# Convolution phases between the sections of attention, transfers of the bias frames on another queue, and part of the ConvFFN's operands made by token tile

## The chip, the cores and the metric

One core of one Trainium2 chip runs the whole layer in one launch. The metric is the device time of that launch in microseconds, from three runs: 1868.3, 1868.54 and 1870.0 us, median 1868.54 us.

## What is computed

One trunk layer over 1024 latent tokens (a grid of 16 rows and 64 columns) and 256 context tokens, 1024 wide, float32. Half of the mixing width is attention with 8 heads, the other half a bidirectional long convolution ("Hyena"). Cut to what matters here:

```python
h = rmsnorm(x, norm1_g) * (1 + sc1) + sh1
proj = h @ w_in                       # q, k, v and three Hyena inputs
a = attend(q, k, v)                   # latent: window 8 x 16 with a bias by
                                      # relative position, and all context keys
x1, x2, v = split(dwconv3(proj[..., 3 * 512:]))
z = x1 * long_conv(v, k_f[0])         # FFT convolution, filters from a small net
hyo = x2 * long_conv(z, k_f[1])
x = x + g1 * (concat(rmsnorm(a), rmsnorm(hyo)) @ w_out)
h2 = rmsnorm(x, norm2_g) * (1 + sc2) + sh2
gate, up = split(dwconv3(h2 @ w_up))  # 2 * 2816 columns
x = x + g2 * ((silu(gate) * up) @ w_down)
y = rmsnorm(x, final_g)
```

## The kernel before

All matrix products of weights run as three products of halves: each float32 operand is split into a rounded high part and the rest (`mm3`, lines 115 to 118). ACT rounds the high part, and DVE or GpSimd (POOL in the profile) subtracts for the low one.

The kernel is written in a framework with tiles and pools. The program emits instructions in its own order; a list scheduler then sets the order on each engine's queue from data dependences and priorities. What is emitted inside `tc.high_priority` is drawn forward by the offset given there. A pool opened with `reuse_waits="tile"` lets each tile start as soon as the old tiles in its place are done with. On the chip each engine and each queue of DMA issues (SP, POOL, ACT) works in order.

The stages, on the time axis of the profile:

- **To some 570 us, filters and input projections.** PE makes the products with w_in (bank `psp`, 512 latent or 256 context columns at a time) for the Hyena inputs, then for q, k and v. Beside them the filters are made on DVE, GpSimd and ACT (helpers at lines 371 to 470; `csl`, `cs`, `GO`, `GE` and `cc` are their tiles), stored as spectra `Kd`. Among the Hyena chunks `rpb_frames` (lines 547 to 558) runs three times: it fills a frame with 16 small loads of the bias table (line 556), reorders it by a copy (557) and stores it to the DRAM table `rpw` (558).
- **448 to 793 us, the convolution** (`chain`, from line 771). Five chains, four for 128 latent channels each and one for the context, of eight phases each: for each of the two convolutions a forward transform on PE (bank `pscA`, line 804, with the table `dftf`; input `s` loaded from `lxd` by line 790), sums of it and the product with the spectrum `K` on DVE, the inverse sums with rotations on ACT and DVE, and the inverse transform (line 876, table `idft`) with the gates. The result goes to the DRAM tensor `hyd`. Two lanes, chains 0, 2, 4 and chains 1, 3, take turns phase by phase. The first 16 phases have three PSUM banks, the other 24 one. All 40 are emitted in a row before the attention, at high priority.
- **597 to 869 us, the attention** (`attend`, from line 1030) for four pairs of heads. Each pair goes through blocks of queries: scores on PE (bank `psS`, line 1047), the bias added with a maximum on DVE (line 1068, tables `tb` 0 to 2), exponentials on ACT, transposes on PE (bank `psX`, line 1091) with evictions on ACT and DVE, and products with the values (bank `psav`, line 1008). The tables of a pair are 48 loads from `rpw` on GpSimd's queue (line 960).
- **880 to 1015 us, the output projection.** w_out is loaded by SP (line 1175, tile `wor`), scaled and split (lines 1167 and 1168). Ten groups of 128 tokens each go through the product with w_out (`omm`, bank `psd`), the residual, the norm and a transpose into `hA` (columns of the first part, 256) and `hB` (the second part, 384) (`post`, line 1315; last multiply at line 1342).
- **From 1015 us, the ConvFFN.** Its product with w_up is a block scheme of seven products in place of eight, with seven sums of w_up's blocks on the left and seven sums `Ta`, `Tb` of blocks of `hA`, `hB` on the right. `first_operands` (line 1347) makes four of the seven steps of the first part inside the loop over token groups; the rest of `Ta` and all of `Tb` come behind the loop (lines 1393 to 1416; subtractions on tiles `T` at line 1233, sums `tsb`). The first sum of w_up's blocks on DVE is line 1478 (tile `S`), and its products go to the banks `psa`, `psb` and `psc`.

The emission of the phases and of the attention before:

```python
for n, i in enumerate(turn2):          # 40 phases in a row
    if n == 16:
        cbk.close()
        cbk = Banks("bkd", "right", "tile", cA=(1, 1))
    with tc.high_priority(offset=CHP):
        next(lanes[i], None)
...
for p_ in range(4):
    attend(p_)
```

Of the kernel before, what the change touches and what calls it, by code (L numbers as in the profile page):

```python
# [19 lines left out]
P = 128  # L20
# [66 lines left out]
def _build(nc, tc, top, V, A, G, T, Q, I, O, dbg, upto):  # L87
# [462 lines left out]
    def rpb_frames(t, var):  # L550
# [214 lines left out]
    Q.dma_start(out=dftf.rearrange("p a b -> p (a b)"), in_=I["t_dft"].flatten().rearrange("(p x) -> p x", p=P))  # L765
    Q.dma_start(out=idft.rearrange("p a b c -> p (a b c)"), in_=I["t_idft"].flatten().rearrange("(p x) -> p x", p=P))
# [135 lines left out]
    turn2 = [0, 0] + [1, 0] * 20 + [0] * 8  # L902
    for n, i in enumerate(turn2):
        if n == 16:
            cbk.close()
            cbk = Banks("bkd", "right", "tile", cA=(1, 1))
        with tc.high_priority(offset=CHP):
            next(lanes[i], None)
# [41 lines left out]

    def bias_load(p_, var):

        for half in range(2):
            for rq in range(8):
# [5 lines left out]
                G.dma_start(out=tv[:, :, a * 8:a * 8 + 64],  # L960
                            in_=rpw[var, :, 2 * p_:2 * p_ + 2, :, d * 8:d * 8 + 64].rearrange("q h u x -> q (h u) x"))
# [9 lines left out]
    for var in range(3):  # L971
        G.memset(tbs[var], NEG)
        bias_load(0, var)
        if var == 0:
            for r in Pring:
                for t in r:
                    G.memset(t[:, 0, :, 11:16], 0.0)
                    G.memset(t[:, 1, :, 0:4], 0.0)

# [50 lines left out]
    def attend(p_):  # L1030

        q, k = qkload(p_) if p_ else first
        vs = tp.tile([P, 12, P], F32, tag="vs", name="vs", bufs=2)
        G.dma_start(out=vs[:, 0:10], in_=vd[:, :, p_ * P:(p_ + 1) * P].rearrange("n p x -> p n x"))
        for h in range(2):
            G.dma_start(out=vs[:, 10:12, h * DH:(h + 1) * DH],
                        in_=I["cache_ctx_v"][0, 0, 2 * p_ + h].rearrange("(n p) d -> p n d", p=P))
        if p_:
            for var in range(3):
                bias_load(p_, var)  # L1040
# [82 lines left out]
        for b in range(2):  # L1123
            l, l2 = stat("l", 8), stat("l2", 8)
            for j in range(2):
                scores(2 * b + j, l, l2, j)
            V.tensor_add(l, l, l2)
            av = bk("av")
            for j in range(2):
# [4 lines left out]
                for vt, ps in local(cb):  # L1134
# [3 lines left out]
                         bs.rearrange("p (b r c) -> p b r c", b=2, r=16))  # L1138
        if p_ < 3:
# [6 lines left out]
    for p_ in range(4):  # L1146
        attend(p_)
# [8 lines left out]
    wsrc = I["w_out"][0].rearrange("(k p) c -> p k c", p=P)  # L1156
    wes = ExitStack()
# [633 lines left out]
```

## Time and profile before

| | |
|---|---|
| median of three runs | 1868.54 us |
| profiled execution | 1868.46 us |
| its span, first to last instruction | 1866.7 us |
| mean granted TensorE clock | 0.963 of full speed |
| PE busy, matmuls | 1728.6 us (93%) |
| DVE busy | 1365.0 us (73%) |
| ACT busy | 891.3 us (48%) |
| POOL busy | 366.3 us (20%) |
| DMA | 249.76 MB, mean 134 GB/s |

The span is what the trace covers; the execution's own time lies 1.8 us above it. PE are matmuls, PEld the loads of their weights, which overlap them. The granted clock is the share of full speed (2.4 GHz) that the chip let TensorE have, averaged over a stretch; the clock has two levels, 1.2 and 2.4 GHz, so 0.75 means half of the stretch at each. SPq and POOL in lists of transfers are the engines that issue them. In rows of waits, "A <- B" reads: A stood idle until B released it.

### The profile page before, as it was taken

The page shows a single profiled execution, that of the slowest core. Times are in us where ns is not written, and L with a number is a line of the kernel's source. Part 1 is how long each engine was busy: PE and PEld are TensorE (multiplying, and loading weights), DVE is VectorE, ACT ScalarE, POOL GpSimd, SP SyncE. Part 2 cuts the span into 40 slices and gives each one's busy share as a digit, 9 for nine tenths or more (in the row PEclk, how much of TensorE's full clock was granted, in tenths as well). Part 3 has the DMA queues.
Part 4 walks back from the last instruction along what each step waited for, and adds up shares of the span by engine and source line. Part 5 has one row for each costly group of instructions (what it writes and reads, how often), then busy time and mean ns, then how long its engine had stood idle before and what let it go on. Part 6 is the DMA issues. An engine that isn't in the chain of part 4 may idle for free.

```text
span 1866.7 us, 27362 instructions
## 1 busy us (share of the span) xinstructions
PE 1728.6 (93%) x9999; PEld 1453.5 (78%) x9999; DVE 1365.0 (73%) x2158; ACT 891.3 (48%) x1852; POOL 366.3 (20%) x436
## 2 busy tenths in 40 slices
PE   5899999999995688988997899999999999999997
PEld 2688778787884445656886899999999999788786
DVE  4668957852987898762466888889878777666797
ACT  4655545443342466673555444344444444443452
POOL 2356656531114555310110000000000000000001
PEclk7999999999997699998999899999999999999999
DMA  7424354356546234331331445554221222844653
GB/s 271 139 77 138 114 164 131 111 138 203 165 141 200 68 99 134 93 111 59 112 113 57 129 151 167 172 169 158 82 66 57 74 74 95 320 141 127 210 191 130
DMA packets 207289, 249.76 MB, mean 134 GB/s; under 512 B 26915, under 2 KB 152980, under 8 KB 206898
## 3 DMA queue, kind: packets, MB, share of 16 engines
q1 hardware_dynamic: 196936, 231.86, 38.5%
q0 software_dynamic: 8512, 15.33, 3.4%
q8 instruction: 79, 1.29, 0.3%
q10 hardware_dynamic: 1705, 0.82, 0.2%
q14 instruction: 57, 0.46, 0.1%
HBM read 176.75 MB, written 71.20 MB: 133 GB/s over the span
## 4 chain that ended last, share of the span: by engine, by line
PE 50%; DVE 22%; DMA 12%; issue 6%; ACT 6%; POOL 2%; SPq 1%; DVEq 0%; ACTq 0%; POOLq 0%
PE psd L116 6%; PE psd L117 6%; PE psd L118 6%; PE psp L116 2%; PE psp L118 2%; PE psp L117 2%; PE psa L116 2%; PE psa L117 2%; PE psa L118 2%; DMA wt<-in_w_down_dram 2%; DMA tdr<-wt 2%; PE psc L117 2%; PE psc L118 2%; PE psc L116 2%; PE psav L1008 1%
## 5 line engine op out<-in xcount | busy, mean ns | idle before, releaser
L116 PE MATMUL psp<-hh,wh 128*128 128x512 f32 (+1 forms) x552 | 201.6, 365 | 1.9 <-ACT wh L121 1.9
L117 PE MATMUL psp<-hl,wh 128*128 128x512 f32 (+1 forms) x552 | 199.0, 361 | 0.0
L118 PE MATMUL psp<-hh,wl 128*128 128x512 f32 (+1 forms) x552 | 198.1, 360 | 0.0
L116 PE MATMUL psa<-T,ws 128*128 128x256 f32 (+1 forms) x528 | 166.0, 314 | 5.6 <-ACT rows L1506 5.4
L117 PE MATMUL psa<-T,ws 128*128 128x256 f32 (+1 forms) x528 | 165.3, 313 | 2.9 <-DVE T L1233 2.9
L1706 POOL TENSOR_TENSOR rs<-rs,mhalf 128x1 f32<-128x1 f32 x10 | 7.7, 770 | 815.3 <-DVE rs L1705 815.3
L118 PE MATMUL psa<-T,ws 128*128 128x256 f32 (+1 forms) x528 | 164.7, 312 | 0.0
L116 PE MATMUL psd<-wd,gs 128*128 128x512 f32 x360 | 140.8, 392 | 3.1 <-ACT gs L121 3.1
L117 PE MATMUL psd<-wd,gs 128*128 128x512 f32 x360 | 141.0, 392 | 0.0
L118 PE MATMUL psd<-wd,gs 128*128 128x512 f32 x360 | 124.9, 390 | 1.8 <-DVE gs L122 1.8
L116 PEld LDWEIGHTS psp<-hh,wh 128*128 128x128 f32 x552 | 104.9, 190 | 22.8 <-issue 7.0
L116 PE MATMUL psc<-T,ws 128*128 128x384 f32 (+1 forms) x352 | 110.0, 313 | 7.8 <-ACT ws L121 7.8
L118 PEld LDWEIGHTS psp<-hh,wl 128*128 128x128 f32 x552 | 104.6, 189 | 15.5 <-issue 1.2
L117 PEld LDWEIGHTS psp<-hl,wh 128*128 128x128 f32 x552 | 105.1, 190 | 14.0 <-issue 0.4
L960 POOL DMA_DIRECT2D tb<-rpw x192 | 100.2, 530 | 78.2 <-DVE m L1068 60.5
L117 PE MATMUL psb<-T,ws 128*128 128x384 f32 (+1 forms) x352 | 109.8, 312 | 0.5 <-DVE T L1233 0.5
L117 PE MATMUL psc<-T,ws 128*128 128x384 f32 (+1 forms) x352 | 110.1, 313 | 0.0
L116 PE MATMUL psb<-T,ws 128*128 128x384 f32 (+1 forms) x352 | 109.4, 311 | 0.4 <-ACT T L1232 0.4
L118 PE MATMUL psc<-T,ws 128*128 128x384 f32 (+1 forms) x352 | 109.7, 312 | 0.0
L118 PE MATMUL psb<-T,ws 128*128 128x384 f32 (+1 forms) x352 | 109.5, 311 | 0.0
L116 PEld LDWEIGHTS psa<-T,ws 128*128 128x128 f32 x528 | 101.1, 192 | 7.4 <-ACT rows L1506 7.4
L117 PEld LDWEIGHTS psa<-T,ws 128*128 128x128 f32 x528 | 101.2, 192 | 3.1 <-DVE T L1233 3.1
(394 smaller groups left out, 4753.1 us busy)
## 6 DMA issues: line engine op xcount, KB each, us to landing
wada<-in_w_ada_dram SPq DMA_DIRECT2D x48, 512.0 KB
wr<-in_w_up_dram SPq DMA_DIRECT2D x44, 512.0 KB
gr<-gdr SPq DMA_DIRECT2D x44, 320.0 KB
wr<-in_w_in_dram SPq DMA_DIRECT2D x23, 512.0 KB
wt<-in_w_down_dram SPq DMA_DIRECT2D x44, 256.0 KB
tdr<-wt SPq DMA_DIRECT2D x44, 256.0 KB
gdr<-cv SPq DMA_DIRECT2D x22, 512.0 KB
wr<-tdr SPq DMA_DIRECT2D x20, 512.0 KB
```

What stands on the lines that cost most here:

```text
L116: T.matmul(out, ah, bh, start=start, stop=False, skip_group_check=True)
L117: T.matmul(out, ah, bl, start=False, stop=False, skip_group_check=True)
L118: T.matmul(out, al, bh, start=False, stop=stop, skip_group_check=True)
L960: G.dma_start(out=tv[:, :, a * 8:a * 8 + 64], in_=rpw[var, :, 2 * p_:2 * p_ + 2, :, d * 8:d * 8 + 64].rearrange("q h u x -> q (h u) x"))
L1008: T.matmul(av[h * DH:(h + 1) * DH, c0:c0 + 256], vt[:, h * DH:(h + 1) * DH], p[:, h * 256:(h + 1) * 256], start=start, stop=False, tile_po ...
L1706: G.tensor_tensor(rs, rs, mhalf, op=ALU.pow)
```

## The change

1. The 51 transfers of `rpb_frames` are issued by GpSimd and not by SP.
2. The loads of the chain's tables `dftf` and `idft` get high priority.
3. Only the first 16 phases of the convolution are emitted in a row at high priority, with three banks. The other 24 are emitted between parts of the attention at ordinary priority: `attend` becomes a generator that stops three times in each pair (after the scores of either half, and after the first half's result), and after the stops two, one and two phases are emitted, after the pair two more; the phases that are left over run out in the last pair. The table of turns is shortened to the 40 phases that there are.
4. All loads of the second pair (`q`, `k`, `vs`, bias tables), and the bias loads of the later pairs, are issued behind the last bias load of the first pair. This sets the order of issue alone.
5. The split halves of the first three of w_out's eight blocks live in a pool `tp0` with two places, `T0` and `T1`. The same places then take `Tb[0]` and `Tb[1]`. Four block sums of the second part are computed 128 columns at a time inside the loop over token groups (`second_sums`, groups 7 to 9), the sum for `Tb[6]` in place; `Tb[0]` and `Tb[1]` are split in the loop too. Behind the loop there remain the splits of `Ta[4]`, `Tb[4]`, `Ta[5]`, `Tb[5]`, `Tb[2]`, `Ta[6]`, `Ta[3]`, `Tb[6]`, `Tb[3]`.

The arithmetic is the same, apart from the tiles of item 5 being smaller. The core of the diff:

```diff
@@ rpb_frames
-            Q.dma_start(out=fv[cq * 8:cq * 8 + 8, :, a:a + 16], in_=I["rpb"][0][:, :, a + 7 - cq:a + 23 - cq])
+            G.dma_start(out=fv[cq * 8:cq * 8 + 8, :, a:a + 16], in_=I["rpb"][0][:, :, a + 7 - cq:a + 23 - cq])
...
-        Q.dma_start(out=rpw[var].rearrange("q h u x -> (q h) (u x)"), in_=g)
+        G.dma_start(out=rpw[var].rearrange("q h u x -> (q h) (u x)"), in_=g)
@@ tables of the chain
+    with tc.high_priority(offset=2000):
+        Q.dma_start(out=dftf..., in_=I["t_dft"]...)
+        Q.dma_start(out=idft..., in_=I["t_idft"]...)
@@ phases
-    turn2 = [0, 0] + [1, 0] * 20 + [0] * 8
-    for n, i in enumerate(turn2):
...
+    turn2 = [0, 0] + [1, 0] * 16 + [0] * 6
+
+    def phases(n):
+        for _ in range(n):
+            if turn2:
+                next(lanes[turn2.pop(0)], None)
+
+    with tc.high_priority(offset=CHP):
+        phases(16)
+    cbk.close()
+    cbk = Banks("bkd", "right", "tile", cA=(1, 1))
@@ attend
+        with tc.issue_after(blast0) if p_ == 1 else ExitStack():
+            q, k = qkload(p_) if p_ else first
...
         if p_:
-            for var in range(3):
-                bias_load(p_, var)
+            with tc.issue_after(blast0):
+                for var in range(3):
+                    bias_load(p_, var)
...
                 scores(2 * b + j, l, l2, j)
+            yield
             V.tensor_add(l, l, l2)
...
+            if b == 0:
+                yield
...
     for p_ in range(4):
-        attend(p_)
+        for n, _ in enumerate(attend(p_)):
+            phases(2 - n % 2)
+        phases(2)
@@ w_out
+    f0s = ExitStack()
+    tp0 = pool(f0s, "Tb0", side="right", reuse_waits="tile")
+    wfirst = [tp0.tile([P, 3, D], F32R, tag=f"T{p}", name=f"w{p}", bufs=1) for p in (0, 1)]
...
-                hi, lo = [wo_.tile([P, D], F32R, tag=f"w{x}{k}", name=f"w{x}{k}", bufs=1) for x in "hl"]
+                hi, lo = [wfirst[i // 3][:, i % 3] for i in (2 * k, 2 * k + 1)] if k < 3 else \
+                    [wo_.tile([P, D], F32R, tag=f"w{x}{k}", name=f"w{x}{k}", bufs=1) for x in "hl"]
@@ operands of the second part
+    def second_sums(t):
+        cs = slice(t * P, (t + 1) * P)
+        if t == 0:
+            ts = acp.tile([P, 3, 4, NS[1]], F32, tag="acc", name="tsb", bufs=1)
+            b.update({4: ts[:, 0], 5: ts[:, 1], 3: ts[:, 2]})
+        V.tensor_sub(b[4][..., cs], b12[..., cs], b11[..., cs])
+        V.tensor_sub(b[5][..., cs], b22[..., cs], b[4][..., cs])
+        V.tensor_sub(b[3][..., cs], b21[..., cs], b[5][..., cs])
+        V.tensor_sub(b12[..., cs], b22[..., cs], b12[..., cs])
...
+        if n >= 7:
+            second_sums(n - 7)
+        if n in (7, 8):
+            Tb[n - 7] = operand(tp0, n - 7, NS[1])
+            osplit(Tb[n - 7], b[n - 7])
...
-    osplit(Tb[0], b[0])
-    osplit(Tb[1], b[1])
-    V.tensor_sub(b[4], b12, b11)
-    a_operand(4)
-    osplit(Tb[4], b[4])
-    V.tensor_sub(b[5], b22, b[4])
-    a_operand(5)
-    osplit(Tb[5], b[5])
-    V.tensor_sub(b[3], b21, b[5])
+    for p in (4, 5):
+        a_operand(p)
+        osplit(Tb[p], b[p])
     osplit(Tb[2], b[2])
-    V.tensor_sub(b[6], b22, b12)
     a_operand(6)
     a_operand(3)
```

Three places where the order on an engine's queue differs. Lines after the change are some 11 to 30 higher than before from the attention on, and one higher in the chain.

**GpSimd, last of the three frames.** Before, between the frame's fill (L552) and its copy (L557) stand filter operations (L394 to L461); the loads are not on this queue:

```order
L552 MEMSET rp 128x480
L455 TENSOR_TENSOR GO<-GO 128x2x2x128
L394 TENSOR_TENSOR cs_2415<-sd_2403,sd_2394 128x512
L395 TENSOR_TENSOR cs_2415<-sd_2403,sd_2394 128x512
L460 TENSOR_TENSOR GE<-cc,GO 128x2x256
L461 TENSOR_TENSOR cc<-cc,GO 128x512
L557 COPY rp<-rp 128x15x4x8
L394 TENSOR_TENSOR cs_2494<-sd_2482,sd_2473 128x512
L395 TENSOR_TENSOR cs_2494<-sd_2482,sd_2473 128x512
```

And after the change:

```order
L552 MEMSET rp 128x480
L556 DMA rp<-in_rpb_dram 8x15x16 x13
L455 TENSOR_TENSOR GO<-GO 128x2x2x128
L556 DMA rp<-in_rpb_dram 8x15x16
L394 TENSOR_TENSOR cs_2415<-sd_2403,sd_2394 128x512
L395 TENSOR_TENSOR cs_2415<-sd_2403,sd_2394 128x512
L556 DMA rp<-in_rpb_dram 8x15x16 x2
L460 TENSOR_TENSOR GE<-cc,GO 128x2x256
L557 COPY rp<-rp 128x15x4x8
L461 TENSOR_TENSOR cc<-cc,GO 128x512
L122 TENSOR_TENSOR wl<-wr,wh 128x1024
L558 DMA rpw<-rp 128x480
```

The 16 loads of the frame (13, then 1, then 2) now stand among the filter operations, 13 of them ahead of `GO`, and the store L558 follows on the same queue.

**PE, first scores of the attention.** `s_...` with `dftf` or `idft` are products of the chain, `psS` scores, `psX` transposes of the attention. Before:

```order
L876 MATMUL pscA<-s_5623,idft 128x256 x4
L1047 MATMUL psS<-k,q 128x264 x2
L1047 MATMUL psS<-k,q 128x288 x2
L804 MATMUL pscA<-s_5863,dftf 128x256 x4
L1047 MATMUL psS<-k,q 128x256 x4
L804 MATMUL pscA<-s_5863,dftf 128x256 x2
L1047 MATMUL psS<-k,q 128x352 x2
L804 MATMUL pscA<-s_5863,dftf 128x256 x2
L1091 MATMUL psX<-ident,pc 128x128 x6
L1047 MATMUL psS<-k,q 128x384 x2
L1091 MATMUL psX<-ident,pc 128x128 x2
L876 MATMUL pscA<-s_5773,idft 128x256 x4
```

And after the change, at the first scores there:

```order
L732 MATMUL pstB<-ident,ck 128x128 x2
L805 MATMUL pscA<-s_5771,dftf 128x256 x8
L1058 MATMUL psS<-k,q 128x264 x2
L1058 MATMUL psS<-k,q 128x288 x2
L877 MATMUL pscA<-s_5623,idft 128x256 x4
L1058 MATMUL psS<-k,q 128x256 x4
L877 MATMUL pscA<-s_5623,idft 128x256 x4
L1058 MATMUL psS<-k,q 128x352 x2
L1102 MATMUL psX<-ident,pc 128x128 x6
L805 MATMUL pscA<-s_6172,dftf 128x256 x2
L1058 MATMUL psS<-k,q 128x384 x2
L1102 MATMUL psX<-ident,pc 128x128 x2
```

In both orders chain products and attention alternate. After the change a transpose of the chain's context keys (L732) and products of other chains stand there, and the phase that follows the scores is one that was emitted between the sections. Counted over the whole queue, 1300 of the 1749 products of `psp` stand ahead of the chain's first product before and 1382 after; 216 of 458 transposes `psX` stand behind the chain's last product before and 112 after.

**DVE, from the last token group to the first sum of w_up's blocks.** L1233 and after the change L1254 are the subtractions of operand splits, `tsb` the block sums, `S` the sum for w_up. Before:

```order
L1402 TENSOR_TENSOR tsb<-hB,tsb 128x1536
L1233 TENSOR_TENSOR T_9376<-hB,T_9376 128x1536
L1405 TENSOR_TENSOR tsb<-hB,tsb 128x1536
L1233 TENSOR_TENSOR T_9377<-hB,T_9377 128x1536
L1233 TENSOR_TENSOR T_9378<-tsb,T_9378 128x1536
L1233 TENSOR_TENSOR T_9380<-hB,T_9380 128x1536
L1233 TENSOR_TENSOR T_9379<-tsb,T_9379 128x1536
L1233 TENSOR_TENSOR T_9415<-tsb,T_9415 128x1536
L1407 TENSOR_TENSOR tsb<-hB 128x1536
L1478 TENSOR_TENSOR S<-wr 128x512
```

And after the change:

```order
L1254 TENSOR_TENSOR T_9402<-hA,T_9402 128x1024
L1393 TENSOR_TENSOR tsb<-hB,tsb 128x4x128
L1395 TENSOR_TENSOR hB<-hB 128x4x128
L1254 TENSOR_TENSOR T_9394<-tsb,T_9394 128x1536
L1394 TENSOR_TENSOR tsb<-hB,tsb 128x4x128
L1254 TENSOR_TENSOR T_9396<-hB,T_9396 128x1536
L1254 TENSOR_TENSOR T_9395<-tsb,T_9395 128x1536
L1254 TENSOR_TENSOR T_9419<-hB,T_9419 128x1536
L1254 TENSOR_TENSOR T_9422<-tsb,T_9422 128x1536
L1508 TENSOR_TENSOR S<-wr 128x512
```

Behind the last group five splits of 128x1536 and one of 128x1024 remain, with tile-wise sums of 128x512 (L1393 to L1395; three more stand a few rows ahead of this excerpt) in place of the sums of 128x1536. `S` stands behind the last split in both.

## Rows read from the trace of the kernel before

**Rows 1.** Page, part 1: busy time, share of span, instructions

```profile
PE 1728.6 (93%) x9999; PEld 1453.5 (78%) x9999; DVE 1365.0 (73%) x2158; ACT 891.3 (48%) x1852; POOL 366.3 (20%) x436
```

**Rows 2.** Windows (start:end, length, busy time) up to the attention's end

```profile
448.00:570.00 122.00, 119.06 (x639) 98.99 (x640) 103.70 (x148) 47.98 (x130) 14.59 (x21) 1.00 0.51 160
570.00:650.00 80.00, 45.88 (x166) 29.47 (x164) 59.81 (x109) 30.74 (x102) 41.63 (x77) 0.67 0.48 132
650.00:750.00 100.00, 85.02 (x496) 50.78 (x492) 89.05 (x194) 64.59 (x213) 52.08 (x98) 0.94 0.42 114
750.00:800.00 50.00, 48.33 (x298) 29.20 (x294) 35.31 (x78) 31.67 (x100) 21.74 (x40) 1.00 0.36 96
800.00:868.00 68.00, 61.28 (x422) 35.28 (x420) 36.87 (x83) 45.02 (x119) 0.00 (x0) 1.00 0.19 62
```

**Rows 3.** Waits, 570 to 650: total, times, longest

```profile
ACT s L812 <- PE pscA L804: 22.3, 4, 12.7
POOL tb L960 <- DVE m L1068: 14.5, 1, 14.5
PE pscA L804 <- DMA s<-lxd: 12.1, 2, 9.9
```

**Rows 4.** Timeline of SP's queue: start, length, line, transfer

```profile
431.40 0.82 SPq L790 DMA_DIRECT2D s<-lxd  x2
...
441.20 0.43 SPq L765 DMA_DIRECT2D dftf<-in_t_dft_dram  x1
```

**Rows 5.** The chain that ended last: start, length, what

```profile
448.76 2.83 PE pscA L804 x12
...
1024.77 8.34 DVE T L1233 x5
```

**Rows 6.** Timeline of PE: start, length, line, tile, form

```profile
554.92 0.40 PE L116 MATMUL psp<-hh,wh 128*128 128x512 f32 x1
555.16 0.39 PE L117 MATMUL psp<-hl,wh 128*128 128x512 f32 x1
...
564.92 0.28 PE L117 MATMUL psp<-hl,wh 128*128 128x256 f32 x1
565.04 0.28 PE L118 MATMUL psp<-hh,wl 128*128 128x256 f32 x1
```

**Rows 7.** Window 400 to 450 (columns as in group 2)

```profile
400.00:450.00 50.00, 44.48 (x251) 36.84 (x251) 8.81 (x16) 11.40 (x28) 7.22 (x7) 1.00 0.68 203
```

**Rows 8.** By tile: count, shortest, median, longest ns

```profile
L960 POOL DMA_DIRECT2D tb<-rpw x192: 528/528/573, 569.5 to 798.9; - x192
...
L556 SPq DMA_DIRECT2D rp<-in_rpb_dram x48: 658/667/1406, 365.6 to 434.7; - x48
...
L399 DVE TENSOR_TENSOR csl<-cs,csh x20: 1201/1220/3227, 108.3 to 395.1; 128x1024 fp32r<-128x1024 f32 x20
```

**Rows 9.** Timelines of PE and DVE, 786 to 872

```profile
791.19 1.89 PE L876 MATMUL pscA<-s,idft 128*128 128x256 f32 x8
...
868.74 0.69 DVE L1137 TENSOR_TENSOR at<-psav,bs 128x512 f32<-128x512 f32 x1 [2.45 <-ACT bs L1025]
```

**Rows 10.** SP's timeline and tile wor: loads and splits of w_out

```profile
798.29 33.42 SPq L1175 DMA_DIRECT2D wor<-in_w_out_dram  x9
...
L1168 DVE SCALAR_TENSOR_TENSOR wl<-wor,vec,wh x9: 744/1278/1285, 803.9 to 837.1; 128x1024 fp32r<-128x1024 f32 x7, 128x512 fp32r<-128x512 f32 x2
```

**Rows 11.** Windows 1003 to 1035 (columns as in group 2)

```profile
1003.00:1015.00 12.00, 5.65 (x29) 4.48 (x28) 6.80 (x12) 8.83 (x15) 1.08 (x2) 0.82 0.22 89
1015.00:1035.00 20.00, 10.60 (x51) 9.26 (x49) 19.96 (x15) 10.59 (x12) 0.00 (x0) 0.76 0.00 0
```

**Rows 12.** Timelines of DVE and PE, 1014 to 1040

```profile
1015.68 0.68 DVE L1342 TENSOR_TENSOR hB<-pst,A 128x512 f32<-128x512 f32 x1
...
1034.82 0.69 DVE L1478 TENSOR_TENSOR S<-wr 128x512 f32<-128x512 f32 x1
...
1037.13 0.58 PE L116 MATMUL psc<-T,ws 128*128 128x256 f32 x1 [7.83 <-ACT ws L121]
```

More of the change, by code (lines that the diff above doesn't have):

```diff
@@ L764, in _build @@
     idft = cp.tile([P, 2, 2, P], F32, name="idft")
-    Q.dma_start(out=dftf.rearrange("p a b -> p (a b)"), in_=I["t_dft"].flatten().rearrange("(p x) -> p x", p=P))
-    Q.dma_start(out=idft.rearrange("p a b c -> p (a b c)"), in_=I["t_idft"].flatten().rearrange("(p x) -> p x", p=P))
+    with tc.high_priority(offset=2000):
+        Q.dma_start(out=dftf.rearrange("p a b -> p (a b)"), in_=I["t_dft"].flatten().rearrange("(p x) -> p x", p=P))
+        Q.dma_start(out=idft.rearrange("p a b c -> p (a b c)"), in_=I["t_idft"].flatten().rearrange("(p x) -> p x", p=P))
     S4B, TB = 3, 1
@@ L901, in _build @@
     lanes = [(None for j in js for _ in chain(j)) for js in ((0, 2, 4), (1, 3))]
-    turn2 = [0, 0] + [1, 0] * 20 + [0] * 8
-    for n, i in enumerate(turn2):
[L904 to L908, printed above, removed]
+    turn2 = [0, 0] + [1, 0] * 16 + [0] * 6
[7 more added lines that the diff above has]
+    cbk = Banks("bkd", "right", "tile", cA=(1, 1))
     for _ in ada:
@@ L949, in _build @@
     tbs[0] = tp.tile([P, NROW * 64], F32, name="tb0")
+    blast = [None]
     def bias_load(p_, var):
@@ L959, in bias_load @@
                 tv = tbs[var][rq * 16:(rq + 1) * 16, HOFF[half]:HOFF[half] + nr * 64].rearrange("q (u x) -> q u x", u=8)
-                G.dma_start(out=tv[:, :, a * 8:a * 8 + 64],
-                            in_=rpw[var, :, 2 * p_:2 * p_ + 2, :, d * 8:d * 8 + 64].rearrange("q h u x -> q (h u) x"))
+                blast[0] = G.dma_start(out=tv[:, :, a * 8:a * 8 + 64], in_=rpw[
+                    var, :, 2 * p_:2 * p_ + 2, :, d * 8:d * 8 + 64].rearrange("q h u x -> q (h u) x")).ins
     def qkload(p_):
@@ L978, in _build @@
                     G.memset(t[:, 1, :, 0:4], 0.0)
+    blast0 = blast[0]
     sel = tp.tile([P, 4, P], F32, name="sel")
@@ L1030, in attend @@
     def attend(p_):
-        q, k = qkload(p_) if p_ else first
+        with tc.issue_after(blast0) if p_ == 1 else ExitStack():
+            q, k = qkload(p_) if p_ else first
         vs = tp.tile([P, 12, P], F32, tag="vs", name="vs", bufs=2)
[L1034 to L1037, printed above, removed]
+        with tc.issue_after(blast0) if p_ == 1 else ExitStack():
+            G.dma_start(out=vs[:, 0:10], in_=vd[:, :, p_ * P:(p_ + 1) * P].rearrange("n p x -> p n x"))
+            for h in range(2):
+                G.dma_start(out=vs[:, 10:12, h * DH:(h + 1) * DH],
+                            in_=I["cache_ctx_v"][0, 0, 2 * p_ + h].rearrange("(n p) d -> p n d", p=P))
         if p_:
-            for var in range(3):
-                bias_load(p_, var)
+            with tc.issue_after(blast0):
+                for var in range(3):
+                    bias_load(p_, var)
         kg = k[:, 0:LL].rearrange("p (u x) -> p u x", u=8)
@@ L1359, in first_operands @@
         yield
+    Tb = [None] * 7
+    b11, b12, b21, b22 = blocks4(hB)
+    b = {0: b11, 1: b21, 2: b22, 6: b12}
+    def second_sums(t):
[7 more added lines that the diff above has]
+        V.tensor_sub(b12[..., cs], b22[..., cs], b12[..., cs])
     for n in range(3):
@@ L1382, in _build @@
     tpb = pool(fbs, "Tb", side="right", reuse_waits="tile")
-    Tb = [None] * 7
-    for p in (0, 1, 4, 5, 2):
+    for p in (4, 5, 2):
         Tb[p] = operand(tpb, p, NS[1])
-    tsb = acp.tile([P, 3, 4, NS[1]], F32, tag="acc", name="tsb", bufs=1)
     a = dict(zip((5, 4, 3, 6), blocks4(hA)))
-    b11, b12, b21, b22 = blocks4(hB)
-    b = {0: b11, 1: b21, 2: b22, 4: tsb[:, 0], 5: tsb[:, 1], 3: tsb[:, 2], 6: tsb[:, 0]}
     def a_operand(p):
@@ L1418, in _build @@
         fbs.close()
+        f0s.close()
         tes.close()
@@ L1573, in _build @@
     fbs.close()
+    f0s.close()
     tes.close()
```

## The prediction

> **What bounds the kernel now.** The sum is made against the profiled execution, 1868.46 us, of which 1866.7 us are the span; the median of the three runs shown is 1868.54 us, so the two can be exchanged. About 3.7 us (0.2%) is what a measurement of this kernel can tell from no change.
>
> The page comes first: PE is busy for 93% of the span and DVE for 73% [rows 1]. That average hides the two stretches which the change touches, so the next view is the busy time by windows [rows 2]. From 448 to 570 us PE is full with the input projections (119.06 of 122 us), and the convolution chain runs beside them and fills DVE for 103.70 us. From 570 on the attention runs beside the rest of the chain, and there PE has only 45.88 busy us of 80 at a granted clock of 0.67, that is for much of the time at 1.2 instead of 2.4 GHz. From 650 to 750 the two engines are nearly level, DVE with 89.05 of 100. From 750 on DVE falls away (35.31 of 50, then 36.87 of 68), while PE does attention almost alone. So between 570 and 868 no engine is full: the heavy DVE work of the chain stands in front, and a tail that DVE hardly needs stands behind.
>
> The waits of 570 to 650 say why [rows 3]: ACT and PE wait for steps of the chain (22.3 us of ACT for chain products, 12.1 us of PE for chain loads), and GpSimd's queue stands 14.5 us before a bias load of the second pair of heads, behind which tables of the first pair are queued. The second place is the start of the ConvFFN: from 1015 to 1035 DVE is busy for 19.96 of 20 us and PE for 10.60 at a granted clock of 0.76 [rows 11], and PE then waits 7.83 us for a block of w_up that DVE makes only after all operands [rows 12].
>
> **Frames to GpSimd's queue, chain tables earlier.** 51 transfers leave SP, 48 of them at 0.667 us each [rows 8], some 32 us of queue time. In front of the chain's start that is what held SP: the chain's first loads went out at 431.40, the table dftf only at 441.20 [rows 4], and the first product ran at 448.76 [rows 5]. The chain does not start earlier for it, though. Counted in PE's order, 1300 projection products stand ahead of the chain's first product before, 1382 after. A product of 512 columns starts every 0.24 us, one of 256 every 0.12 us [rows 6]; two thirds are of the first kind, so 82 take (2 x 0.24 + 0.12)/3 x 82 = 16 us. PE idled 5.5 us between 400 and 450 [rows 7], most of which I expect back: the start moves by 16 - 5 = 11 us, to 460.
>
> On GpSimd the frames' price is that of the nearest transfers which it issues, the 192 bias loads at 0.528 us [rows 8]: 51 x 0.53 = 27 us of a queue with time to spare. The frames also stand in front of filter work there, 16 of them (8.5 us) before the last operations of a filter. The chain cannot start before the filters are done; its first loads would move from 431 to 440, and with some 5 us to land they still beat 460. So I cost this at nothing, hidden by the projections; with that cover gone it would be 8.5 us. Its other end is below nothing: without the queue on SP the chain could start at 448 as now, 12 us better.
>
> **Bias loads in order.** The loads of the second pair of heads now stand behind the last table of the first pair. The 14.5 us wait goes from in front of the first pair's tables. What is late next is DVE, which in the old order had chain work there anyway; so this has no term of its own and is part of the share taken below.
>
> **Phases between the sections.** No arithmetic is removed from the attention or the chain: DVE has 103.70 + 59.81 + 89.05 + 35.31 + 36.87 = 324.7 us to do from 448 to 868 [rows 2]. What moves is where it stands. Three stretches:
>
> - Beside the projections: the same 103.7 us in the same 122 us, from 460 to 582. Two more chain groups of about half a phase slip behind the projections' end in the new order; they are small against the bounds.
> - The tail after the chain's last product. Counted in PE's order 216 products of psX (of 458) follow it before, 112 now. Before, they take from 793.1 to 868.7, 75.6 us [rows 9]; 112 of them take 39 us. In that time DVE has the splits of w_out, 10.5 us (seven of 1.28 and two of 0.74) [rows 10], and 112/216 of the other 26.4 us of the last window, 13.7 us, in all 24.2 us.
> - Between the two: 324.7 - 103.7 - 24.2 = 196.8 us of DVE. How dense can it run? The bounds are rows of the same mixture: 0.75 (570 to 650) and 0.89 (650 to 750) [rows 2]. I take 0.89, since there both kinds of work are at hand, as they are in the new order to the end, and the 570 row has waits for loads that now go out in order. PE is no nearer limit there: it had 85 us beside DVE's 89. That gives 221 us, from 582 to 803.
>
> The end of the attention comes at 803 + 39 = 842 instead of 868.7: 27 us. With 0.75 it would be 262 us and 883, 14 us later than now. The price of the ends is thus -27 to +14, and what decides is DVE's share.
>
> Nine loads and splits of w_out wait for the chain's space. Before they ran from 798 to 837, 39 us [rows 10]; the tail is now 39 us and the first product with w_out needs only the first four blocks, some 12 us further on. Hidden; if the cover fails, up to 8 us.
>
> **Second part's operands.** Before, from the last group's multiply to the first sum for w_up DVE works 1034.82 - 1015.68 = 19.1 us without a gap [rows 12]: ten operations of 128x1536 at 1.67 us (five took 8.34) [rows 5], one of 128x1024 and two small ones. In the new order five of 128x1536 stand there, one of 128x1024 (1.1) and six of 128x512 at 0.6 (the first row of [rows 12] is one): 8.35 + 1.1 + 3.6 = 13.1 us. That saves 6.0, not 19, because that w_up sum still stands behind the last operand. Of the work brought forward, 4.8 us of slices stand among the last two groups' chains, where DVE had 12 - 6.8 = 5.2 us free [rows 11]; I let them delay the last group by 2 us. The net is -4; the bounds are -12 (the sum and PE's 7.83 both go) and +2. The shared buffers of w_out add no transfer.
>
> The sum: 1868.5 - 26.5 - 4 = **1838 us**.
>
> **One rule against the change.** In the trace DVE and GpSimd do get in each other's way: one kind of DVE subtraction takes 1.20 us at best and 3.23 us at worst [rows 8], while the 192 transfer issues on GpSimd lie between 528 and 573 ns although DVE was 75 to 89% busy around them [rows 2, 8]. The Trainium skill, SBUF — State Buffer, section "SBUF: two separate sides", warns that descriptors of transfers issued by GpSimd cannot be written while DVE holds the port pair that the two share, and its section "A bandwidth-pool intuition that's wrong" gives 3.1 us in place of 0.62; by that the 51 frames would take some 158 us, an estimate from that page. The 528 to 573 ns speak against it here. As a mechanism of this kernel its price is worked out from rows: 16 issues in front of the filters' last work, each longer by what the slowest subtraction lost, 2.0 us, delay it by 32 + 8.5 = 40 us; the chain's loads go out at 471 instead of 431, land at 476 or so, and the chain starts some 17 us after my 460. That gives 1855.
>
> **Rivals.**
>
> - *Denser and earlier*: SP's free queue lets the chain start at 448, and DVE runs at 0.90, just above the 0.89 of its best row, which makes 196.8/0.90 = 219 us of the middle stretch; the attention ends at 570 + 219 + 39 = 828, and the operands give 8. That is 1868.5 - 41 - 8 = 1820, rounded. For it: dftf was late by 10 us [rows 4]. Against it: PE's order.
> - *Nothing gained in the middle*: DVE runs at 0.79, 249 us, the end is 870, and only the operands count: 1866. For it: over 570 to 800 DVE's average today is already 184.2/230 = 0.80 [rows 2].
> - *Slower: the chain and the attention in lockstep.* Every queue is in order, the chain has one PSUM bank, and now each phase stands between attention parts on PE, ACT and DVE; each chain step that is late holds the attention behind it, as ACT's 22.3 us and PE's 12.1 us of waits show [rows 3]. If the whole middle runs at the 0.75 of that stretch, the end is 883 and the time 1868.5 + 14.5 - 4 = 1879. It is slower than now as soon as the share falls under 0.79.
> - *Frames starve behind DVE*: 1855, as above.
>
> **How the numbers follow.** My case (shares from 0.84 to 0.92, 1830 to 1853) gets 0.48; denser and earlier 0.15; frames starved 0.09; nothing gained 0.11; lockstep 0.17. Faster by over 0.2% is the first three, 0.72; within 0.2% is 0.11; slower 0.17. The range reaches from 1810, below the dense case, to 1872, which leaves out most of lockstep and the far end of the dense case with earlier operands.
>
> **What would show it.** Right: the chain's first product near 460; the windows between 580 and 800 with DVE near 0.89 throughout and PE's granted clock near 1.0; the last chain product some 39 us before the attention's end, near 842; the frames' issues at about 0.53 us; the first sum for w_up some 13 us after the last group's multiply. Wrong: chain products that wait for loads or PSUM in the middle (lockstep), frame issues of 1 us and more, products of w_out that wait for its splits, or an attention that ends after 860.

## The result and the profile after

| kernel | median, us | ratio to before, 95% interval |
|---|---|---|
| before (4 runs) | 1868.94 | |
| the change (4 runs) | 1857.33 | 0.9945 [0.9928, 0.9962] |
| the change again (6 runs, beside other kernels) | 1855.38 | 0.9944 [0.9927, 0.9962] |

The change makes the kernel faster by 0.55%, some 10.4 us (0.0055 to 0.0056 of 1868). The forecast was 30 us: right in sign and inside the range, but three times too large.

The two traces, by what happens when (starts, in us from the start of the span; the pairs' ends are DVE's last multiplies into `at`):

| | before | after | difference |
|---|---|---|---|
| chain's first product | 448.8 | 457.9 | +9.1 |
| last projection product | 567.2 | 559.9 | -7.3 |
| second pair of heads done | 784 | 757 | -27 |
| chain's last product starts | 792.7 | 830.8 | +38.1 |
| attention's last multiply | 868.7 | 864.7 | -4.0 |
| first w_up product (`psa`) | 1015.1 | 1014.1 | -1.0 |
| first product that needs a w_up sum (`psc`) | 1037.1 | 1029.2 | -7.9 |
| last `psa` product | 1583.6 | 1573.3 | -10.3 |
| end of the span | 1866.7 | 1857.7 | -9.0 |

The row of the page's first part, and the attention's end, which answer to [rows 1] and [rows 9], and the multiplies that end the second pair, before and after:

```profile
PE 1723.9 (93%) x9999; PEld 1453.9 (78%) x9999; DVE 1368.3 (74%) x2166; ACT 892.5 (48%) x1852; POOL 396.3 (21%) x487
```

```profile
829.72 1.46 PE L877 MATMUL pscA<-s,idft 128*128 128x256 f32 x6
...
864.68 0.69 DVE L1149 TENSOR_TENSOR at<-psav,bs 128x512 f32<-128x512 f32 x1 [1.79 <-ACT bs L1033]
```

```profile
784.08 0.42 DVE L1118 TENSOR_TENSOR at<-psav,bs 128x256 f32<-128x256 f32 x1
```

```profile
756.54 0.39 DVE L1129 TENSOR_TENSOR at<-psav,bs 128x256 f32<-128x256 f32 x1
```

So the attention gave 4 us, the way from there to the ConvFFN cost 3, its start gave 6.9, and the rest of the ConvFFN up to its last `psa` product 2.4, which is within what that stretch varies by (last section). Behind that product 1.3 us were lost again. The row that surprises is the third: the second pair is done 27 us earlier, the very size of the forecast, and 23 of the 27 are gone when the attention ends.

The same five windows of the changed kernel as in [rows 2] (busy time and count for PE, weight loads, DVE, ACT and GpSimd, then the granted clock, the DMA share and GB/s):

```profile
448.00:570.00 122.00, 115.21 (x599) 95.12 (x598) 88.20 (x130) 46.45 (x127) 20.63 (x34) 0.97 0.50 156
570.00:650.00 80.00, 47.07 (x194) 27.87 (x196) 63.26 (x122) 33.69 (x116) 45.87 (x85) 0.72 0.50 139
650.00:750.00 100.00, 88.84 (x550) 54.47 (x546) 87.54 (x193) 66.43 (x220) 38.52 (x73) 0.97 0.33 92
750.00:800.00 50.00, 42.91 (x251) 26.51 (x252) 40.26 (x86) 30.42 (x95) 23.86 (x44) 0.90 0.47 127
800.00:868.00 68.00, 59.45 (x388) 36.98 (x388) 42.68 (x85) 42.45 (x104) 0.72 (x1) 1.00 0.27 86
```

DVE is far from the forecast 0.89 throughout: 63.26 of 80 (0.79, before 0.75), 87.54 of 100 (0.88, before 0.89) and 40.26 of 50 (0.81, before 0.71). Some DVE work has moved from before 570 to behind 750, which answers to the later chain. PE has not filled its weak stretch: 47.07 of 80 us where it was 45.88.

### The profile page after: what moved, and what is told of

Its sections match the earlier page's. It is cut to its first block, busy times and chain, and to the rows that moved or that the text cites. A ratio compares the mean times of both kernels' runs of the same rounds, so it can differ in the third digit from the quotient of the medians.

```text
span 1857.7 us, 27350 instructions
## 1 busy us (share of the span) xinstructions
PE 1723.9 (93%) x9999; PEld 1453.9 (78%) x9999; DVE 1368.3 (74%) x2166; ACT 892.5 (48%) x1852; POOL 396.3 (21%) x487
## 4 chain that ended last, share of the span: by engine, by line
PE 54%; DVE 19%; DMA 13%; ACT 5%; issue 5%; POOL 3%; SPq 0%; DVEq 0%; ACTq 0%; POOLq 0%
PE psd L116 5%; PE psd L117 5%; PE psd L118 5%; PE psp L116 4%; PE psp L118 4%; PE psp L117 4%; DMA wt<-in_w_down_dram 3%; PE psa L116 2%; PE psa L117 2%; PE psa L118 2%; DMA tdr<-wt 2%; PE psc L118 2%; PE psc L117 2%; PE psc L116 2%; PE psb L117 1%
```

## The experiments

All intervals are 95%. Items are those of the list of the change. Where a time in us stands for a ratio, it is the ratio's distance from 1 times 1868.

**The operands alone** (item 5), and **all but the operands** (items 1 to 4).

```diff
+    tp0 = pool(f0s, "Tb0", side="right", reuse_waits="tile")
...
+        if n >= 7:
+            second_sums(n - 7)
+        if n in (7, 8):
+            Tb[n - 7] = operand(tp0, n - 7, NS[1])
+            osplit(Tb[n - 7], b[n - 7])
...
```

> The kernel before with item 5 of the change alone (w_out's first three blocks in the shared places, second part's operands by token tile). The trace of the changed kernel has the last ConvFFN product of psa 10.3 us earlier than before, its first one 1.0 us earlier, so some 9 us came between the two. Theory A (the operands give nearly all of the gain, the order of the chain little): 8 to 9 us faster than before, 1860 us. Theory B (the prediction's price of 4 us for the operands is right, the rest comes from the order and is spoiled by another part): 4 us faster, 1865 us.

> The whole change but for item 5. Theory A: what is left is the 4 us by which the attention ended earlier in the changed kernel, less nothing: 1865 us. Theory B: 7 to 8 us faster than before, 1861 us. If the shared places of w_out hold up the attention's tail (its splits ran to 867 us there, behind the last chain product), this kernel has an attention that ends clearly before 864 us.

Measured: the operands alone 0.9959 [0.9945, 0.9972], 7.7 us faster; the rest 0.9991 [0.9977, 1.0006], not to be told from no change. Both are nearer to Theory A. In the trace of the operands alone the attention ends at 867.4, 1.3 us earlier than before, the first `psc` product follows the first `psa` product by 15.1 us where it was 22.0, and the stretch between the attention's end and the first `psa` product is 148.5 us where it was 146.4. In the rest alone the attention ends at 860.7, 8 us earlier, so its trace shows a gain of which the median keeps 1.7 us; the ConvFFN and the down projection gave 3.3 us back there. That difference stays open, the more so since items 3 and 4 without the frames, and items 1, 2 and 4 without the phases, come out at 0.9958 and 0.9956 below. The shared places of w_out don't cost the attention's tail anything that shows: from the chain's last product to the last multiply it is 33.7 us here and 33.9 in two traces of the whole change, and the 3 to 4 us by which this attention ends earlier (860.7 against 864.7 and 863.7) are there at its first scores already (584.5 against 588.9 and 588.7).

**The phases alone** (item 3), and **the phases with the bias loads in order** (items 3 and 4).

```diff
...
     for p_ in range(4):
-        attend(p_)
+        for n, _ in enumerate(attend(p_)):
+            phases(2 - n % 2)
+        phases(2)
```

> The kernel before with item 3 alone (24 phases between the sections of the attention, frames still on SP, bias loads in the old order). Theory A (order of emission moves little): between 1864 and 1870 us. Theory B (the phases give the forecast 27 us and the frames on GpSimd or the late start of the chain take them back): 1842 to 1850 us.

> Items 3 and 4 on the kernel before (phases between sections, loads of the second pair behind the last bias load of the first pair). Theory A: 1864 to 1868 us, within 2 us of the kernel with item 3 alone. If the 14.5 us that GpSimd's queue waited before a bias load of the second pair are on the path in the new order, it is 5 us or more faster than the kernel with item 3 alone.

Measured: 1.0012 [1.0000, 1.0024] and 0.9958 [0.9945, 0.9971]. The item to which the prediction gave 27 of its 30 us gives nothing by itself, and the item to which it gave no term is worth 10 us beside it.

**The change without the frames' move** (items 3 to 5), **the frames alone** (items 1 and 2), **the order of the bias loads alone** (item 4), and the whole change again.

```diff
...
         if p_:
-            for var in range(3):
-                bias_load(p_, var)
+            with tc.issue_after(blast0):
+                for var in range(3):
+                    bias_load(p_, var)
```

> The changed kernel without items 1 and 2 (the bias frames' transfers back on SP, chain tables at ordinary priority). In the changed kernel's trace GpSimd's last filter work came 14 to 17 us later than before, the chain's first loads 20 us and its first product 9 us. Theory A (items 1 and 2 cost time): the 7.6 us of the operands and the 8.9 us of items 3 and 4 add up, 16 us faster than before, 1852 to 1854 us, and some 4 us or more faster than the whole change. Theory B (the later chain start is paid back, since PE no longer idles 5.5 us before it and the projections end 7 us earlier): within 2 us of the whole change, 1857 us.

> Items 1 and 2 alone on the kernel before (frames' transfers on GpSimd, chain tables at high priority). Theory A: slower than before by 3 to 8 us, 1872 to 1877 us, the chain starting near 458. Theory B: within 2 us of before.

> Item 4 alone on the kernel before (loads of the second pair behind the last bias load of the first pair; phases still in a row). Items 3 and 4 together came out at 0.9958, item 3 alone at 1.0012. Theory A (the bias loads' order is what frees the start of the attention, whatever the order of the phases): 7 to 10 us faster than before, 1859 to 1862 us. Theory B (it counts only where the phases stand between the sections): within 3 us of before.

> The whole change once more, on the chip of the three runs beside it: 0.993 to 0.996 of before, 1856 to 1861 us, as in its first measurement.

Measured: without the frames' move 0.9946 [0.9929, 0.9964], the frames alone 0.9963 [0.9947, 0.9979], the bias order alone 0.9960 [0.9944, 0.9975], the whole change 0.9944. Both theories on the frames were wrong for the frames alone: alone they give 6.9 us, in the whole change nothing that can be told (0.9946 without them, 0.9944 with them). And three parts that give 7 to 8 us each do not give 22. Something is removed more than once.

The traces also show where the new order on PE comes from. The chain's last product starts at 793.0 us with the phases alone, as before (792.7), at 806.3 with phases and bias order, and at 826.3 with the frames alone, where no phase was moved. Of the 520 `psX` products in each trace, 258 start behind it before and with the phases alone, 146 with the frames alone, and 142 in the change. So the shorter tail that the prediction gave to the phases came mostly with the frames' move, by way of the order that the scheduler then chose. The rows of the last products, phases alone and frames alone:

```profile
791.51 1.89 PE L876 MATMUL pscA<-s,idft 128*128 128x256 f32 x8
```

```profile
824.70 1.99 PE L877 MATMUL pscA<-s,idft 128*128 128x256 f32 x8
```

GpSimd's own waits from 570 to 616 us say what is removed twice. The views are the waits of that queue, first the phases alone (no gain), then the frames alone (a gain):

```profile
POOL tb L964 <- DVE m L1072: 14.2, 1, 14.2
```

```profile
POOL tb L961 <- DMA tb<-rpw: 2.3, 2, 1.4
...
POOL tb L961 <- DVE m L1069: 0.3, 1, 0.3
```

The stall before a bias load [rows 3] is still 14.2 us with the phases alone, and 14.3 us with the operands alone. With the frames alone it is 0.3 us: the chain starts later there (461.6 in place of 448.8) and the bias loads earlier (558.3 in place of 569.5), and the order on GpSimd's queue is another: 48 bias loads go out ahead of the first that waits for DVE, where before the 17th waited. With the bias order alone, none of them waits for DVE in that stretch. The timeline of GpSimd's queue there shows the first pair's loads, and behind them those of the second pair, with gaps of 2.5 us at most:

```profile
585.98 5.21 POOL L962 DMA_DIRECT2D tb<-rpw  x10 [0.92 <-DMA vs<-vd]
591.86 5.95 POOL L962 DMA_DIRECT2D tb<-rpw  x11 [0.67 <-DMA tb<-rpw]
...
604.44 0.57 POOL L967 DMA_DIRECT2D q<-qd  x1
```

Before, this queue stood still from 595 to 609.58 us. The first pair's first half was done at 679 before, at 664 with the bias order alone, at 651 with the frames alone; the attention ended at 868.7, 857.1 and 866.2. So in the trace of the frames alone 28 us at the first pair leave 2.5 at the attention's end, and 3.1 us more come in the ConvFFN, whose code is the same: how the 6.9 us of that run come about is shown only in part.

**Three combinations and the tail**: bias order and operands (items 4 and 5), the change without the phases (items 1, 2, 4 and 5), frames and bias order (items 1, 2 and 4), and the whole change with one block of w_out split in place of eight.

```diff
     for k in range(KC):
+        if k:
+            wo.append(wo[0])
+            continue
```

> Items 4 and 5 on the kernel before (bias loads in order, operands by token tile; phases in a row, frames on SP). Theory A (the gain of the whole change is one stall of GpSimd's queue before the first pair's tables, 7 to 8 us, and the operands, 4 to 7 us; the phases between the sections give nothing): 12 to 15 us faster than before, 1852 to 1855 us, no slower than the whole change. Theory B (the phases between the sections carry part of the gain): 3 us or more slower than the whole change, 1859 us or more.

> The whole change without item 3 (all 40 phases in a row at high priority). Theory A: as fast as the whole change or up to 5 us faster, 1851 to 1857 us; DVE from 580 to 700 us busy for over 0.85 of the time, where the whole change has 0.80. Theory B: 3 us or more slower than the whole change.

> Items 1, 2 and 4 on the kernel before (frames on GpSimd, chain tables early, bias loads in order; phases in a row, operands as before). Items 1 and 2 alone came out at 0.9963, item 4 alone at 0.9960. If each removes the same stall of GpSimd's queue in the start of the attention (Theory A), together they give it once: 0.995 to 0.997, 1857 to 1861 us. If they are separate gains (Theory B), they add: 0.992, 1851 to 1853 us.

> The whole change with one block of w_out loaded and split in place of eight (all eight products with w_out use the first block's halves: seven loads and splits are left out, the products stay). In the whole change w_out's splits ran from 841.6 to 866.9 us, in the last 34 us of the attention. If they hold the tail (Theory B), the attention ends 4 to 8 us earlier against the chain's last product than the 33.2 us of the whole change, and the time is that much shorter; if they are hidden (the prediction's cost of nothing, Theory A), under 2 us.

Measured: items 4 and 5 alone 0.9939 [0.9921, 0.9958], 11.4 us faster; without the phases 0.9938 [0.9923, 0.9954]; frames and bias order 0.9956 [0.9939, 0.9973]; one block of w_out 0.9949 [0.9932, 0.9967]. So two items, the order of the bias loads and the operands, give all that the whole change gives, and leaving the phases in a row costs nothing. Frames and bias order together give what either gives alone: they remove the same stall, as Theory A had it; in their traces the 14.5 us of that wait are 0.3 us with the frames, none with the bias order and 1.9 with both. Behind the bias order the operands add less than alone: 2 to 4 us by these ratios (0.9939 against 0.9960, 0.9946 against 0.9958, 0.9938 against 0.9956), which is within the noise of each pair. The splits of w_out in the tail are hidden but for a few us at most: without seven of eight the last multiply of the attention comes 30.1 us behind the start of the chain's last product in place of 33.9, just short of Theory B's 4 to 8, but the chain's last product comes 3.6 us later there, the attention ends at 864.5 against 864.7 and 863.7, and the time is no shorter.

One number of Theory A was wrong: without the phases DVE is busy for 97.91 of the 120 us from 580 to 700, 0.82, not over 0.85. The same window in the change, with the bias order alone, and in the kernel before, one each:

```profile
580.00:700.00 120.00, 88.92 (x446) 53.04 (x447) 95.48 (x205) 66.01 (x223) 51.21 (x95) 0.83 0.38 107
```

```profile
580.00:700.00 120.00, 91.36 (x468) 55.47 (x467) 104.34 (x220) 66.34 (x224) 57.85 (x107) 0.85 0.42 120
```

```profile
580.00:700.00 120.00, 81.58 (x375) 48.96 (x375) 99.78 (x199) 57.71 (x198) 57.81 (x107) 0.77 0.42 117
```

The bias order alone made DVE denser in this stretch (104.34 us, against 99.78 before), and PE with it (91.36 against 81.58). The phases between the sections made DVE thinner there where they came on top of other items (101.35 us beside the bias order; 95.48 in the change, against 97.91 without them), and not by themselves (102.00).

**Which engine decides.** Nineteen microseconds taken out of DVE alone, or out of PE alone, in either order of the phases.

```diff
-                V.tensor_sub(Ys[:, h, 0], Ys[:, h, 0], B[:, 0])
-                V.tensor_add(Ys[:, h, 1], Ys[:, h, 1], B[:, 1])
+                if j < 2:
+                    V.tensor_sub(Ys[:, h, 0], Ys[:, h, 0], B[:, 0])
+                    V.tensor_add(Ys[:, h, 1], Ys[:, h, 1], B[:, 1])
...
```

```diff
-                for vt, ps in local(cb):
-                    av_mm(av, 256 * j, vt, ps, False)
+                for u, (vt, ps) in enumerate(local(cb)):
+                    if not (p_ and u):
+                        av_mm(av, 256 * j, vt, ps, False)
```

> The whole change with DVE work left out of chains 2 to 4: the last two sums of each product with the spectrum and the last two of each inverse first stage, 32 operations of 128x512 (0.60 us apart in the trace), 19 us of DVE, all behind 582 us; PE, ACT and transfers stay. Theory D (the prediction's step: DVE's share decides the stretch from 582 us to the attention's end): the attention ends 14 to 19 us earlier than the 864 us of the whole change. Theory P (PE is the limit there, at 0.88 to 0.90 of the time in the last two pairs): under 7 us earlier, since DVE is off the path.

> The whole change with PE work left out of the last three pairs: the products with the values of all local key blocks but the first of each group of queries, 30 calls at 0.63 us (384 records took 60.3 us, 96 calls), 19 us of PE; transposes, their evictions, DVE and ACT stay. Theory P: the attention ends 14 to 21 us earlier than in the whole change (864 us). Theory D: under 7 us earlier.

> The kernel before with the same 32 DVE operations left out (19 us, between 582 and 793 us). If DVE's share set the middle before (Theory D): the attention ends 14 to 19 us earlier than 868.7 us. If PE and the stall of GpSimd's queue set it (Theory P): under 7 us earlier.

> The kernel before with the same 30 calls of products with the values left out (19 us of PE in the last three pairs, 20 of them in the last two, which run from 784 to 869 us with PE busy for 0.90). Theory P: the attention ends 12 to 21 us earlier than 868.7 us. Theory D, where only the tail of some 75 us behind the chain is PE's: 8 to 13 us.

| 19 us less of | ratio to before | second pair done | attention's last multiply |
|---|---|---|---|
| the change as it is | 0.9944 | 757 | 864.7, 863.7 |
| DVE, in the change | 0.9892 [0.9864, 0.9920] | 746 | 850.7 |
| PE, in the change | 0.9902 [0.9873, 0.9931] | 755 | 853.3 |
| the kernel before as it is | 1 | 784 | 868.7 |
| DVE, in the kernel before | 0.9987 [0.9969, 1.0005] | 778 | 865.0 |
| PE, in the kernel before | 0.9936 [0.9914, 0.9958] | 784 | 862.7 |

The last multiplies of the attention, with less of DVE and with less of PE in the change, then the same two in the kernel before:

```profile
850.74 0.69 DVE L1151 TENSOR_TENSOR at<-psav,bs 128x512 f32<-128x512 f32 x1 [1.79 <-ACT bs L1035]
853.25 0.69 DVE L1150 TENSOR_TENSOR at<-psav,bs 128x512 f32<-128x512 f32 x1 [0.35 <-ACT bs L1033]
```

```profile
865.01 0.69 DVE L1139 TENSOR_TENSOR at<-psav,bs 128x512 f32<-128x512 f32 x1 [2.45 <-ACT bs L1027]
862.72 0.69 DVE L1138 TENSOR_TENSOR at<-psav,bs 128x512 f32<-128x512 f32 x1 [1.48 <-ACT bs L1025]
```

Neither theory has it alone. In the change some 13.5 of 19 us of DVE come back at the attention's end. Of the 32 operations 22, or 13 us, stood ahead of the second pair's end, and 11 us are back by then; the 6 us behind it gave 2.5. Of the 19 us of PE 11 come back: 2 of the 6 us that lay in the second pair, and 9 of the 13 in the last two pairs. The times of these runs are 9.7 and 7.8 us below the change's 0.9944, a little less than the traces and within the intervals. So DVE is most of the path through the first half of the stretch, and PE through the second, and neither is all of it. ACT, busy for 68.52 of the 109 us of the last two pairs (next section), was not tested in this way.

In the kernel before it stays open which engine decides. By the times DVE's 19 us are worth 2.4 us (0.9987, under 6 by the interval) and PE's 12. At the attention's end the traces have 3.7 us for DVE, as Theory P had it, and 6.0 for PE, less than either theory, although the projections ended 4.9 and 3.4 us later there than in the trace of before; and of PE's 12 us some 4.9 lie in the ConvFFN, which the edit doesn't touch.

## Why the prediction was wrong

**The step that failed** is "Between the two: 324.7 - 103.7 - 24.2 = 196.8 us of DVE. How dense can it run?", with its choice of 0.89 and the sentence that "PE is no nearer limit there". Over the forecast stretch, 582 to 803 us, the window of the changed kernel reads:

```profile
582.00:803.00 221.00, 179.30 (x1001) 109.49 (x1001) 181.57 (x387) 128.44 (x418) 99.72 (x186) 0.89 0.39 107
```

That is 0.82 of DVE, where the kernel before has 179.38 of the same 221 us, 0.81. PE has 179.30 us, before 175.61. The order of emission moved work, and made neither engine much denser. What was done earlier in the first two pairs was paid for in the last two. The windows from the end of the second pair to the attention's end, in the change and before:

```profile
757.00:866.00 109.00, 95.45 (x598) 58.57 (x596) 74.95 (x152) 68.52 (x189) 19.28 (x37) 0.95 0.33 97
```

```profile
784.00:870.00 86.00, 77.37 (x523) 45.07 (x521) 47.22 (x104) 55.83 (x148) 12.48 (x24) 1.00 0.27 80
```

Two pairs take 109 us in place of 86, for 95.45 us of PE in place of 77.37: a share of 0.88 and 0.90. Of the 18 us more of PE, 14.5 are chain products that used to be done by then (6.28 us of `dftf` and 12.00 us of `idft` products, against 3.78 before). The prediction read PE's 85 us beside DVE's 89 as no nearer limit. In the 16 traces that leave PE's work as it is, PE was busy for 0.87 to 0.92 of the last two pairs and never more, and of the 13 us of its work that were taken out there in the change 9 came back: there PE was most of the limit. That the idle rest comes from steps that go to and fro between engines is an argument, and no run shows it. For the forecast the share counts for 20 of the 23 us by which the attention ended later than 842 (worked out below, beside the projections).

**The second step that failed** is "this has no term of its own" for the bias loads. The 14.5 us stall was priced at nothing by what DVE did meanwhile. By itself item 4 is worth 7.5 us (0.9960 [0.9944, 0.9975]), half of the stall, and the rows had shown the reason: the stall stood in front of tables which the first pair's scores need, and everything of that pair comes behind them.

The other steps, in their order:

- *Frames and tables, chain's start*: the start at 457.9 answers to the forecast 460, and PE filled its idle time, as expected (50.00 of the 50 us from 400 to 450). But what set it was not only PE's order. The issues took 0.62 us, not 0.53. The last sums `cs` of a filter on GpSimd came at 405.2 in place of 387.8, its last operation at 415.2 in place of 401.4, and the chain's first loads went out at 451.1 in place of 431.4: a delay of 20 us where 8.5 had been worked out. In the whole change the net is nothing that can be told, as costed (0.9946 without the frames' move). The row of the 48 issues, and SP's timeline, which answers to [rows 4]:

```profile
L556 POOL DMA_DIRECT2D rp<-in_rpb_dram x48: 609/619/719, 364.2 to 428.0; - x48
```

```profile
445.39 0.34 SPq L489 DMA_DIRECT2D Kc<-GO  x1
...
450.70 0.36 SPq L766 DMA_DIRECT2D dftf<-in_t_dft_dram  x1
451.11 0.49 SPq L791 DMA_DIRECT2D s<-lxd  x1
```

  `Kc<-GO`, the store of the last filter, went out at 425.60 before.

- *The rule against the change*: issues of 3.1 us did not occur; the longest was 0.719 us, with DVE busy for 37.95 of the 65 us from 364 to 429. The Trainium skill gives that figure, in the section "A bandwidth-pool intuition that's wrong" of SBUF — State Buffer, for a transfer beside a DVE `tensor_copy`. Beside these 48 issues DVE ran TENSOR_TENSOR and SCALAR_TENSOR_TENSOR operations and one copy of 0.17 us out of PSUM, so these issues don't test the rule, and the prediction priced all 51 by it without that condition. The rival's 1855 us is near the measured time by luck: the chain's first product was at 457.9, and not 17 us behind 460.
- *The tail*: 34 us from the chain's last product to the last multiply, where 39 were forecast; w_out's splits in it are hidden but for a few us at most.
- *Beside the projections*: wrong, and nearly without effect on the end. The 82 products that moved ahead of the chain's start no longer stand behind it: the start came 9.1 us later and the projections' end 7.3 us earlier, 16.4 in all, as the 82 were priced. So the projections ended at 560, and not at 582. DVE did 79 us of work beside them, not 103.7, and 223.59 us were left for the middle, not 196.8:

```profile
458.00:560.00 102.00, 99.00 (x524) 81.65 (x524) 79.22 (x113) 38.66 (x106) 10.90 (x6) 1.00 0.45 145
560.00:831.00 271.00, 215.13 (x1200) 133.20 (x1199) 223.59 (x468) 155.45 (x506) 117.98 (x228) 0.87 0.39 106
```

  At 0.89 these 223.59 us would have taken 251 us and the attention would have ended at 560 + 251 + 34 = 845, near the forecast 842. They took 271 (0.83): the share alone is 20 of the 23 us by which the end came later.
- *The operands*: right in the work between the group and the sum. From the last group's multiply to the first w_up sum 13.1 us were forecast:

```profile
1014.69 0.68 DVE L1363 TENSOR_TENSOR hB<-pst,A 128x512 f32<-128x512 f32 x1
...
1026.11 1.75 DVE L1254 TENSOR_TENSOR T<-tsb,T 128x1536 fp32r<-128x1536 f32 x1
1027.78 0.68 DVE L1508 TENSOR_TENSOR S<-wr 128x512 f32<-128x512 f32 x1
```

  It is 13.09 us from the first to the last start. PE's wait for that sum remains, as said, if shorter than the 7.83 us of [rows 12]:

```profile
1029.17 0.58 PE L116 MATMUL psc<-T,ws 128*128 128x256 f32 x1 [6.03 <-ACT ws L121]
```

  `psc` follows `psa` by 6.9 us less, and the way to `psa` is 2.1 to 3.3 us longer in the traces with item 5 that leave no work out, where 2 were forecast: net 4 us by the traces, as forecast, and 7.7 [5.2, 10.3] by the times of item 5 alone.
- *The rivals*: "Nothing gained in the middle" (0.11) named what happened to the phases. Its DVE share of 0.79 to 0.80 and the measured 0.82 belong together; what it lacked was the bias order. By the forecast's own sum 0.79 gives 1866 us, so the change would be slower than before only under some 0.78, not 0.79 as the lockstep rival says.

## What to carry to other kernels

A share of busy time from one stretch is no price for another: before counting on it, ask which engine takes over when the first gets its work earlier, and whether that engine has room for it in the stretch behind. Where an in-order queue of transfers stands still in front of loads that the first step of a stage needs, the stall can count even while other engines are busy: here 7.5 us of 14.5. Parts of a change that each give the same gain alone may be removing one and the same wait; only the runs with two of them together tell.

## What the runs showed of the hardware

The same code in the ConvFFN, from the first `psc` product to the last `psa` product, took between 541.5 and 549.1 us over the 18 traces, although no run changes that code. The granted clock was 1.00 from 1060 to 1560 us in four of them (before, after, and those with the longest and the shortest time there). PE's waits for ACT's evictions there were 5.4, 2.7, 4.8 and 1.7 us in these four. The kernel before took 1860.5 to 1876.5 us in the 33 runs beside the first four experiments, against 1868.3 to 1870.0 in the four runs of the first table: differences under 3 us could be told only from many runs, or from the traces by stage.
